# Decay between positions of a gated DeltaNet from differences of cumulative sums, in place of masked products and scans

## The chip, the cores and the metric

The kernel runs on one core of a Trainium2 chip. The metric is device time in microseconds (us) of one execution. The profile calls the engines PE (TensorE, matrix products), DVE (VectorE), ACT (ScalarE), POOL (GpSimd) and SP (SyncE, which here issues the transfers).

## What is computed

One layer of a streaming encoder block in float32: SEQ = 1024 positions, D_MODEL = 1024, batch 1. A modulated norm and one input projection feed a gated DeltaNet (8 heads of 128), a latent attention (8 heads) and branch gates; both are merged and projected, and a gated MLP with a short convolution follows. The change lies in the DeltaNet:

```python
gc = jnp.cumsum(chunks_s(g), axis=-1)
decay = jnp.exp(jnp.where(tri, gc[..., :, None] - gc[..., None, :], -jnp.inf))
a_mat = jnp.where(strict, jnp.einsum('bhncd,bhnjd->bhncj', k_beta, kc) * decay, 0.0)
...
intra = jnp.where(tri, jnp.einsum('bhncd,bhnjd->bhncj', qc, kc) * decay, 0.0)
k_dec = kc * jnp.exp(gc[..., -1:] - gc)[..., None]
```

`g` is at most 0, one number a position and head. Between two positions c and j of a chunk, what is remembered decays by exp(gc[c] - gc[j]), the exponential of the sum of g over the positions after j up to c. `a_mat` takes it where c > j, `intra` where c >= j.

## The kernel before

The kernel works in NB = 8 blocks of 128 positions, a head's decays being one tile G of 128x1024 (partition: position j of the block; columns: block and position c). Products on TensorE that must be exact are made as three passes over parts `_h` and `_l` of each operand.

The parts that matter here, in the order of time. Up to about 100 us inputs are normed and the first three heads of keys k0 to k2 are projected. Then, from 100 to 262 us, `k_dense` projects keys k3 to k7 (the loop over heads in `conv_proj`: tile `kNx` is the copy of the product out of PSUM, `kNa` the convolution of width 4, three scalar_tensor_tensor on VectorE at L402 and a SiLU on ScalarE), `decay_rates` computes g, beta and exponentials of its sums, and `k_post`, once for each head in two interleaved streams, transposes the keys (`kNt`, copied to `ktN` at L572), takes their norms (`sse`, `nrm`, `wst`, `nws`), calls `decay`, scales `kt` for the state update (`kdw`), stores it, and multiplies the Gram matrix kk by `nws` and G into `nB` (L591). `nB` is stored to DRAM (`bd_d`), and `inverse` loads all heads' diagonal blocks as X and inverts them in 62 pairs of VectorE instructions (L616, L618). Gate projections (`gt`, weights `gNw`, results `gst` through a sigmoid on ScalarE, L679) fill TensorE from about 200 us.

From 440 to 775 us the query heads follow. `d_prep` prepares a head: it calls `decay` again, and multiplies the Gram matrix kq by `wst` and G into `att`. `d_scan` runs the recurrence over the 8 blocks: ks (state times keys), R on VectorE (L795), y on TensorE and its copy on VectorE (L801), su and the new state S (L808, L810). From about 820 us on the attention, the merge and the MLP follow, without the decays.

`decay` as it stands: g of the head is sent to all partitions by a transfer, POOL multiplies by the mask m_gt (1 where c > j, else 0), VectorE sums along each block in 8 scans, ScalarE takes the exponential, and POOL masks the result, by m_gt for the keys and by m_ge (c >= j) for the queries. It is called 16 times. The tile G has one buffer in the query part; in the key part odd heads use the two buffers of another tag.

TensorE's order is fixed by `PEOrder`, a planner of streams with costs and due times; each product is pinned behind the one before. It gives the same order before and after, but for the one product on gT. All other engines' orders come from the scheduler of the Tile framework, which simulates the program; they are not written by hand. An engine runs its instructions in order.

Of the kernel before, what the change touches and what calls it, by code (L numbers as in the profile page):

```python
# [16 lines left out]
P = 128  # L17
# [97 lines left out]
def _body(tc, nc, ctx, A, out):  # L115
# [22 lines left out]
    def gtt(o, a, b, op):  # L138
        nc.gpsimd.tensor_tensor(o, a, b, op=op)  # L139
# [46 lines left out]


    ident = pc.tile([P, P], F32, name="ident")
    m_gt = pc.tile([P, P], F32, name="m_gt")
    m_ge = pc.tile([P, P], F32, name="m_ge")  # L190
    for m, pat, mul, cmp in ((ident, -1, 1, ALU.is_equal), (m_gt, 1, -1, ALU.is_gt), (m_ge, 1, -1, ALU.is_ge)):
        nc.gpsimd.memset(m, 1.0)
        nc.gpsimd.affine_select(out=m, in_=m, pattern=[[pat, P]], compare_op=cmp, fill=0.0, base=0,
                                channel_multiplier=mul)
    ones = pc.tile([P, P], F32, name="ones")
    nc.vector.memset(ones, 1.0)
# [261 lines left out]
    def bcast_row(src, n, name, pool_):  # L458
# [5 lines left out]
    hb = [P, NH, NB]  # L464
    beta, g, egc, negc, egl, nrm, wst, nws, sse = [
        po.tile(hb, F32, name=n) for n in ("beta", "g", "egc", "negc", "egl", "nrm", "wst", "nws", "sse")]
    g_d = dr.tile([NH, S], F32, name="g_d")

    def decay_rates():
        nea = bcast_row(A["dn_a_log"], NH, "nea", po)  # L470
        dtb = bcast_row(A["dn_dt_bias"], NH, "dtb", po)
        nc.scalar.activation(nea, nea, AF.Exp)
        yield ((("sm",),), 0.4)
        gs = po.tile([P, 5, NH, NB], F32, tag="sq", bufs=2, name="gs")
        al, e_, s_, z_, q_ = [gs[:, i] for i in range(5)]
        V = nc.vector
        V.tensor_tensor(al, albe[:, 0], dtb.unsqueeze(2).broadcast_to(hb), op=ALU.add)
        V.scalar_tensor_tensor(e_, al, -1.0, al, op0=ALU.mult, op1=ALU.min)
        nc.scalar.activation(e_, e_, AF.Exp)
        nc.scalar.activation(beta, albe[:, 1], AF.Sigmoid)  # L480
        V.tensor_scalar(s_, e_, 2.0, None, op0=ALU.add)
        V.reciprocal(s_, s_)
        V.tensor_tensor(s_, s_, e_, op=ALU.mult)
        V.tensor_tensor(z_, s_, s_, op=ALU.mult)
        V.tensor_scalar(q_, z_, 1.0 / 17.0, None, op0=ALU.mult)
        for d in (15, 13, 11, 9, 7, 5, 3):
            V.scalar_tensor_tensor(q_, q_, 1.0 / d, z_, op0=ALU.add, op1=ALU.mult)
        V.scalar_tensor_tensor(q_, q_, 1.0, s_, op0=ALU.add, op1=ALU.mult)
        V.tensor_scalar(al, al, 0.0, None, op0=ALU.max)
        V.scalar_tensor_tensor(q_, q_, 2.0, al, op0=ALU.mult, op1=ALU.add)  # L490
        V.scalar_tensor_tensor(g, q_, -1.0, nea.unsqueeze(2).broadcast_to(hb), op0=ALU.mult, op1=ALU.mult)
        gf = g.rearrange("p h b -> p (h b)")
        yield 8.0
        t = bank("tp", "gT")
        pe.tr(t[0:HB, 0:P], gf, ident)
        gT = po.tile([HB, P], F32, tag="sq", bufs=2, name="gT")
        nc.vector.tensor_copy(gT, t[0:HB, 0:P])
        nc.sync.dma_start(g_d.rearrange("h (b p) -> (h b) p", p=P), gT)
        t = bank("tp", "gcum")
        pe.mm(t[:, 0:HB], m_ge, gf)  # L500
        nc.scalar.activation(egc.rearrange("p h b -> p (h b)"), t[:, 0:HB], AF.Exp)
        V.tensor_scalar(negc, egc, -1.0, None, op0=ALU.mult)
        t = bank("tp", "gall")
        pe.mm(t[:, 0:HB], ones, gf)
        nc.scalar.activation(egl.rearrange("p h b -> p (h b)"), t[:, 0:HB], AF.Exp)
        pe.at[("g",)] = pe.t - CONV + 2.0

# [17 lines left out]
        nc.scalar.activation(sq, t, AF.Square)  # L525
        nc.vector.tensor_reduce(dst[:, hf * 4:hf * 4 + 4], sq.rearrange("p (j d) -> p j d", d=P), axis=AX.X, op=ALU.add)

    def decay(h, name, tag="G", bufs=1):
        G = po.tile([P, NB, P], F32, tag=tag, bufs=bufs, name=f"{name}G{h}")
        nc.sync.dma_start(G.rearrange("p b t -> p (b t)"), g_d[h:h + 1, :].broadcast_to([P, S]))  # L530
        gtt(G, G, m_gt.unsqueeze(1).broadcast_to([P, NB, P]), ALU.mult)
        for b in range(NB):
            nc.vector.tensor_tensor_scan(G[:, b, :], m_gt, G[:, b, :], 0.0, ALU.mult, ALU.add)
        nc.scalar.activation(G, G, AF.Exp)
        return G

    def mask_mul(G, m):
        gtt(G, G, m.unsqueeze(1).broadcast_to([P, NB, P]), ALU.mult)

    def gram(a, b, name):  # L540
        for hf in range(2):
# [21 lines left out]
    def k_post(par):  # L563
        for h in range(par, NH, 2):
            yield ((("k", h), ("g",)), CONV + 4.9 * h * (h < NS))
            kf = kfs[h]
            nc.sync.dma_start(kf_d[h], kf)
            kt = po.tile([P, NB, P], F32, tag="kd", bufs=2, name=f"kt{h}")

            def k_use(hf, t):  # L570
                sumsq(sse[:, h], hf, t, f"k{h}")
                nc.vector.tensor_copy(kt[:, hf * 4:hf * 4 + 4, :].rearrange("p j d -> p (j d)"), t)  # L572

            yield from tok_major(kf, f"k{h}", k_use)
            nc.vector.tensor_scalar(sse[:, h], sse[:, h], EPS, None, op0=ALU.add)
            nc.gpsimd.tensor_tensor(nrm[:, h], sse[:, h], phalf[:, 0:NB], op=ALU.pow)
            nc.vector.reciprocal(wst[:, h], sse[:, h])
            nc.vector.tensor_tensor(wst[:, h], wst[:, h], beta[:, h], op=ALU.mult)
            nc.vector.tensor_scalar(nws[:, h], wst[:, h], -1.0, None, op0=ALU.mult)
            G = decay(h, "k", *(("vn", 2) if h % 2 else ("G", 1)))  # L580
            kdw = po.tile([P, NB], F32, name=f"kdw{h}", tag="kdw", bufs=2)
            nc.vector.tensor_tensor(kdw, wst[:, h], G[:, :, P - 1], op=ALU.mult)
            gtt(kt, kt, kdw.unsqueeze(2).broadcast_to([P, NB, P]), ALU.mult)
            nc.sync.dma_start(kt_d[h], kt.rearrange("p b d -> p (b d)"))
            mask_mul(G, m_gt)
            nB = po.tile([P, NB, P], F32, tag="att", bufs=2, name=f"nB{h}")
            yield 4.0 if h < NS else 4
            for hf, t in gram(kf, kf, f"kk{h}"):
                for j in range(4):
                    b = hf * 4 + j  # L590
                    nc.vector.scalar_tensor_tensor(nB[:, b, :], t[:, j * P:(j + 1) * P], nws[:, h, b:b + 1], G[:, b, :],  # L591
                                                   op0=ALU.mult, op1=ALU.mult)
                yield
            for i in range(2):
                o = slice(i * 64, i * 64 + 64)
                nc.sync.dma_start(bd_d[h, :, i].rearrange("b j c -> j b c"), nB[o, :, o])
            nc.sync.dma_start(b12_d[h], nB[0:64, :, 64:128])
            pe.mark("pk", h)
# [117 lines left out]
    def d_prep():  # L716
        for h in range(NH):
# [48 lines left out]
                pe.mm(t[0:64, b * 64:b * 64 + 64], TW[64:128, b, :], U[64:128, b, 64:128])  # L766
            (nc.scalar.copy if 3 & 2 else nc.vector.tensor_copy)(U[0:64, :, 64:128], t[0:64, :].rearrange("p (b c) -> p b c", c=64))
            yield
            G = decay(h, "q")
            mask_mul(G, m_ge)  # L770
            att = d["att"] = po.tile([P, NB, P], F32, tag="att", bufs=2, name=f"att{h}")
            for hf, t in gram(kf, qf, f"kq{h}"):
                for j in range(4):
# [1055 lines left out]
```

## Time and profile before

| what | value |
|---|---|
| median of 3 runs (lowest to highest) | 2211.99 us (2209.98 to 2216.24) |
| profiled execution | 2214.16 us |
| its span, from first to last instruction | 2212.2 us |
| mean granted TensorE clock | 0.980 |
| busy: PE, DVE, ACT, POOL | 95%, 62%, 41%, 37% |

The profiled execution is 2.2 us above the median, and 1.96 us longer than its span. Shares of busy time are averages over stages with different limits; which engine an engine waits for in a stage is read from the waits and timelines there. The granted clock is 1.00 at 2.4 GHz and 0.50 at 1.2 GHz.

### The profile page before, as it was taken

The numbers are of one execution on the slowest core, as the hardware profiler recorded it, in microseconds if no ns is written. First come the engines' busy times: TensorE is split into PE (matmuls) and PEld (weight loads), VectorE is DVE, ScalarE is ACT, GpSimd is POOL, SyncE is SP. The second block draws the span as 40 slices with busy tenths as digits, with TensorE's granted clock in tenths as the row PEclk, the third lists the DMA queues.
The fourth block names the chain that finished last, engine by engine and source line by source line (L and its number), as shares of the span: only waits on it lengthen the run. The fifth ranks groups of instructions, "written<-read, shape, count | busy, mean of one in ns | idle before, by whom it ended". The sixth has DMA issues, their size and how long they took to land.

```text
span 2212.2 us, 30724 instructions
## 1 busy us (share of the span) xinstructions
PE 2093.9 (95%) x11525; PEld 1805.5 (82%) x11525; DVE 1377.9 (62%) x2212; ACT 902.4 (41%) x1822; POOL 812.4 (37%) x574
## 2 busy tenths in 40 slices
PE   7978899999999998899998999999999999999999
PEld 6866788878888898888877888898778888878887
DVE  7589499465555527658638886636575555555554
ACT  5644322463554522325324564236443333433221
POOL 1057420131212212427437770226554444442231
PEclk8989999999999999999999999999999999999999
DMA  9445633425223327578754446423322222244644
GB/s 281 125 137 155 168 112 90 138 76 154 91 86 102 99 77 240 175 247 285 240 153 138 121 119 204 148 77 115 115 96 86 86 82 81 96 144 146 219 143 147
DMA packets 277460, 309.30 MB, mean 140 GB/s; under 512 B 38895, under 2 KB 218428, under 8 KB 277056
## 3 DMA queue, kind: packets, MB, share of 16 engines
q1 hardware_dynamic: 277312, 307.35, 44.8%
q8 instruction: 90, 1.47, 0.3%
q14 instruction: 58, 0.48, 0.1%
HBM read 223.63 MB, written 83.66 MB: 139 GB/s over the span
## 4 chain that ended last, share of the span: by engine, by line
PE 60%; DVE 15%; DMA 7%; issue 3%; POOL 3%; ACT 2%; SPq 0%; POOLq 0%; ACTq 0%; DVEq 0%
PE d L63 11%; PE gt L63 5%; PE m L63 5%; PE my L63 4%; PE mx L63 4%; PE yb L63 4%; PE wo L63 4%; PE qt L63 3%; PE v L63 3%; PE q L63 3%; DVE lt L616 3%; DVE X L618 3%; PE s L63 2%; PE mz L63 2%; DMA wada<-in_w_ada 2%
## 5 line engine op out<-in xcount | busy, mean ns | idle before, releaser
L63 PE MATMUL d<-wd,gh 128*128 128x512 f32 x704 | 217.3, 390 | 2.2 <-DVE wd L151 1.7
L63 PEld LDWEIGHTS d<-wd,gh 128*128 128x128 f32 x704 | 132.1, 188 | 30.8 <-DVE wd L151 2.5
L63 PE MATMUL d<-wd,gl 128*128 128x512 f32 x352 | 137.0, 389 | 0.0
L139 POOL TENSOR_TENSOR wdr<-wdr,gf 128x512 f32<-128x512 f32 x44 | 68.8, 1565 | 164.0 <-DMA wdr<-in_ffn_w_down 157.6
L151 DVE TENSOR_TENSOR gl<-gr,gh 128x1024 fp32r<-128x1024 f32 x44 | 56.4, 1283 | 106.3 <-ACT gh L143 104.2
L143 ACT CAST gh<-gr 128x1024 fp32r<-128x1024 f32 x44 | 46.3, 1054 | 153.4 <-PE d L63 152.9
L63 PEld LDWEIGHTS d<-wd,gl 128*128 128x128 f32 x352 | 66.1, 188 | 13.8
L1236 ACT ACTIVATE P<-s,nm 128x512 f32<-128x512 f32 (+2 forms) x96 | 55.2, 581 | 51.7 <-DVE nm L1234 43.4
L136 POOL TENSOR_SCALAR P<-P,sm 128x896 f32<-128x896 f32 (+4 forms) x64 | 49.4, 780 | 63.1 <-DVE nm L1234 17.5
L139 POOL TENSOR_TENSOR acc<-acc,vv 128x512 f32<-128x512 f32 x44 | 64.5, 1486 | 20.0 <-ACT acc L1764 12.6
L616 DVE TENSOR_TENSOR lt<-X 128x62 f32<-128x62 f32 (+30 forms) x62 | 61.7, 996 | 9.1 <-issue 7.1
L151 DVE TENSOR_TENSOR wd<-wdr,wd 128x512 fp32r<-128x512 f32 x44 | 64.4, 1466 | 1.5 <-ACT wd L143 1.5
L1118 DVE SCALAR_TENSOR_TENSOR ada<-wada,sc,ada 128x1024 f32<-128x1024 f32 x28 | 41.5, 1481 | 35.3 <-DMA wada<-in_w_ada 35.1
L63 PE MATMUL mz<-T2h,wP 128*128 128x512 f32 x176 | 58.3, 392 | 3.2 <-ACT wP L143 2.1
L618 DVE TENSOR_TENSOR X<-X,lt 128x62 f32<-128x62 f32 (+30 forms) x62 | 59.5, 959 | 2.0
L1259 ACT CAST PTh<-pT 128x512 fp32r<-128x512 f32 (+2 forms) x96 | 45.9, 483 | 36.4 <-PE pT L66 36.0
L66 PE MATMUL pT<-ident,P 128*128 128x128 f32 x288 | 49.0, 280 | 11.2 <-DVE PTl L1260 8.2
L63 PE MATMUL m<-B21h,wP 128*128 128x512 f32 x176 | 58.9, 396 | 0.0
L63 PE MATMUL my<-T4h,wP 128*128 128x512 f32 x176 | 57.9, 390 | 0.9 <-DVE vv L1752 0.9
L63 PE MATMUL mx<-B22h,wP 128*128 128x512 f32 x176 | 57.9, 390 | 0.0
L63 PE MATMUL my<-T3h,wP 128*128 128x512 f32 x176 | 57.8, 389 | 0.0
L63 PE MATMUL m<-B11h,wP 128*128 128x512 f32 x176 | 57.5, 389 | 0.0
(1427 smaller groups left out, 7356.1 us busy)
## 6 DMA issues: line engine op xcount, KB each, us to landing
gr<-gg_d SPq DMA_DIRECT2D x44, 512.0 KB
wada<-in_w_ada SPq DMA_DIRECT2D x32, 512.0 KB
gg_d<-acc SPq DMA_DIRECT2D x22, 512.0 KB
wdr<-in_ffn_w_down SPq DMA_DIRECT2D x44, 256.0 KB
x<-in_x SPq DMA_DIRECT2D x16, 512.0 KB
ad<-in_w_ada SPq DMA_DIRECT2D x16, 512.0 KB
sg_d<-gst SPq DMA_DIRECT2D x32, 256.0 KB
q_d<-qst SPq DMA_DIRECT2D x48, 128.0 KB
```

The costliest lines, as they stand in the source:

```text
L63: self._pin(self.nc.tensor.matmul(out, lhsT, rhs, start=start, stop=stop, skip_group_check=more), cost)
L66: self._pin(self.nc.tensor.transpose(out=out, in_=in_, identity=ident), 0.107)
L136: return nc.gpsimd.tensor_scalar(o, i, by, 0.0, op0=ALU.mult, op1=ALU.add)
L139: nc.gpsimd.tensor_tensor(o, a, b, op=op)
L143: nc.scalar.copy(hi, src)
L151: return nc.vector.tensor_tensor(lo, src, hi.bitcast(F32), op=ALU.subtract)
L616: nc.vector.tensor_tensor(tv, X[:, 0:k, k:k + 1].broadcast_to([P, k, n]), X[:, k:k + 1, k + 1:64].broadcast_to([P, k, n]), op=ALU.mult)
L618: nc.vector.tensor_tensor(X[:, 0:k, k + 1:64], X[:, 0:k, k + 1:64], tv, op=ALU.add)
L1118: nc.vector.scalar_tensor_tensor(acc, raw, sc[:, k:k + 1], acc, op0=ALU.mult, op1=ALU.add)
L1236: nc.scalar.activation(Pt[:, kc], o, AF.Exp, bias=nm[:, 0:1], accum_out=sm[:, b:b + 1])
L1259: nc.scalar.copy(dh, tv)
```

## The change

g_d, from which the rows are sent to all partitions, now holds the cumulative sums: the product that made the transpose of g now has m_ge in place of the identity. A new tile `gc` holds the same sums by partition. `decay` subtracts gc of position j from the row and takes the minimum with a floor tile, in one scalar_tensor_tensor for each block on VectorE: `f_gt` is 0 where c > j and -10000 elsewhere, `f_ge` likewise for c >= j; after the exponential the masked places are 0. POOL's products with the masks and VectorE's scans go. The decay to a block's end, for `kdw`, comes from a new small tile `kde`, not from G's last column. `f_ge` lies in the tile `albe`, which is free by then; POOL fills it in two instructions.

```diff
--- before.py
+++ after.py
@@ -186,11 +186,12 @@
 
 
     ident = pc.tile([P, P], F32, name="ident")
-    m_gt = pc.tile([P, P], F32, name="m_gt")
+    f_gt = pc.tile([P, P], F32, name="f_gt")
     m_ge = pc.tile([P, P], F32, name="m_ge")
-    for m, pat, mul, cmp in ((ident, -1, 1, ALU.is_equal), (m_gt, 1, -1, ALU.is_gt), (m_ge, 1, -1, ALU.is_ge)):
-        nc.gpsimd.memset(m, 1.0)
-        nc.gpsimd.affine_select(out=m, in_=m, pattern=[[pat, P]], compare_op=cmp, fill=0.0, base=0,
+    for m, pat, mul, cmp, v_in, v_out in ((ident, -1, 1, ALU.is_equal, 1.0, 0.0), (f_gt, 1, -1, ALU.is_gt, 0.0, -1e4),
+                                          (m_ge, 1, -1, ALU.is_ge, 1.0, 0.0)):
+        nc.gpsimd.memset(m, v_in)
+        nc.gpsimd.affine_select(out=m, in_=m, pattern=[[pat, P]], compare_op=cmp, fill=v_out, base=0,
                                 channel_multiplier=mul)
     ones = pc.tile([P, P], F32, name="ones")
     nc.vector.memset(ones, 1.0)
@@ -464,6 +465,8 @@
     hb = [P, NH, NB]
     beta, g, egc, negc, egl, nrm, wst, nws, sse = [
         po.tile(hb, F32, name=n) for n in ("beta", "g", "egc", "negc", "egl", "nrm", "wst", "nws", "sse")]
+    gc, kde = [po.tile(hb, F32, name=n) for n in ("gc", "kde")]
+    f_ge = albe.rearrange("p a h b -> p (a h b)")
     g_d = dr.tile([NH, S], F32, name="g_d")
 
     def decay_rates():
@@ -492,16 +495,22 @@
         gf = g.rearrange("p h b -> p (h b)")
         yield 8.0
         t = bank("tp", "gT")
-        pe.tr(t[0:HB, 0:P], gf, ident)
+        pe.mm(t[0:HB, 0:P], gf, m_ge)
         gT = po.tile([HB, P], F32, tag="sq", bufs=2, name="gT")
         nc.vector.tensor_copy(gT, t[0:HB, 0:P])
         nc.sync.dma_start(g_d.rearrange("h (b p) -> (h b) p", p=P), gT)
         t = bank("tp", "gcum")
         pe.mm(t[:, 0:HB], m_ge, gf)
         nc.scalar.activation(egc.rearrange("p h b -> p (h b)"), t[:, 0:HB], AF.Exp)
+        nc.vector.tensor_copy(gc.rearrange("p h b -> p (h b)"), t[:, 0:HB])
         V.tensor_scalar(negc, egc, -1.0, None, op0=ALU.mult)
         t = bank("tp", "gall")
         pe.mm(t[:, 0:HB], ones, gf)
+        V.tensor_tensor(kde.rearrange("p h b -> p (h b)"), t[:, 0:HB], gc.rearrange("p h b -> p (h b)"), op=ALU.subtract)
+        nc.scalar.activation(kde, kde, AF.Exp)
+        nc.gpsimd.memset(f_ge, 0.0)
+        nc.gpsimd.affine_select(out=f_ge, in_=f_ge, pattern=[[1, P]], compare_op=ALU.is_ge, fill=-1e4, base=0,
+                                channel_multiplier=-1)
         nc.scalar.activation(egl.rearrange("p h b -> p (h b)"), t[:, 0:HB], AF.Exp)
         pe.at[("g",)] = pe.t - CONV + 2.0
 
@@ -525,17 +534,14 @@
         nc.scalar.activation(sq, t, AF.Square)
         nc.vector.tensor_reduce(dst[:, hf * 4:hf * 4 + 4], sq.rearrange("p (j d) -> p j d", d=P), axis=AX.X, op=ALU.add)
 
-    def decay(h, name, tag="G", bufs=1):
+    def decay(h, name, floor, tag="G", bufs=1):
+
         G = po.tile([P, NB, P], F32, tag=tag, bufs=bufs, name=f"{name}G{h}")
         nc.sync.dma_start(G.rearrange("p b t -> p (b t)"), g_d[h:h + 1, :].broadcast_to([P, S]))
-        gtt(G, G, m_gt.unsqueeze(1).broadcast_to([P, NB, P]), ALU.mult)
         for b in range(NB):
-            nc.vector.tensor_tensor_scan(G[:, b, :], m_gt, G[:, b, :], 0.0, ALU.mult, ALU.add)
+            nc.vector.scalar_tensor_tensor(G[:, b, :], G[:, b, :], gc[:, h, b:b + 1], floor, op0=ALU.subtract, op1=ALU.min)
         nc.scalar.activation(G, G, AF.Exp)
         return G
-
-    def mask_mul(G, m):
-        gtt(G, G, m.unsqueeze(1).broadcast_to([P, NB, P]), ALU.mult)
 
     def gram(a, b, name):
         for hf in range(2):
@@ -577,12 +583,11 @@
             nc.vector.reciprocal(wst[:, h], sse[:, h])
             nc.vector.tensor_tensor(wst[:, h], wst[:, h], beta[:, h], op=ALU.mult)
             nc.vector.tensor_scalar(nws[:, h], wst[:, h], -1.0, None, op0=ALU.mult)
-            G = decay(h, "k", *(("vn", 2) if h % 2 else ("G", 1)))
+            G = decay(h, "k", f_gt, *(("vn", 2) if h % 2 else ("G", 1)))
             kdw = po.tile([P, NB], F32, name=f"kdw{h}", tag="kdw", bufs=2)
-            nc.vector.tensor_tensor(kdw, wst[:, h], G[:, :, P - 1], op=ALU.mult)
+            nc.vector.tensor_tensor(kdw, wst[:, h], kde[:, h], op=ALU.mult)
             gtt(kt, kt, kdw.unsqueeze(2).broadcast_to([P, NB, P]), ALU.mult)
             nc.sync.dma_start(kt_d[h], kt.rearrange("p b d -> p (b d)"))
-            mask_mul(G, m_gt)
             nB = po.tile([P, NB, P], F32, tag="att", bufs=2, name=f"nB{h}")
             yield 4.0 if h < NS else 4
             for hf, t in gram(kf, kf, f"kk{h}"):
@@ -766,8 +771,7 @@
                 pe.mm(t[0:64, b * 64:b * 64 + 64], TW[64:128, b, :], U[64:128, b, 64:128])
             (nc.scalar.copy if 3 & 2 else nc.vector.tensor_copy)(U[0:64, :, 64:128], t[0:64, :].rearrange("p (b c) -> p b c", c=64))
             yield
-            G = decay(h, "q")
-            mask_mul(G, m_ge)
+            G = decay(h, "q", f_ge)
             att = d["att"] = po.tile([P, NB, P], F32, tag="att", bufs=2, name=f"att{h}")
             for hf, t in gram(kf, qf, f"kq{h}"):
                 for j in range(4):
```

The lists below print instructions in the order of an engine's program: line, operation, output, inputs, columns; head numbers stand in names (`kG1` is the key decay of head 1), the last number is the tile's own. Scans are printed as SCALAR_TENSOR_TENSOR too; line 533 tells them.

VectorE in the key part, around `nB` of head 1. Before:

```order
L582 TENSOR_TENSOR kdw1_1226<-wst_700,kG1_1214 128x8
L151 TENSOR_TENSOR k7w_l_1623<-k7w_r_1620,k7w_h_1622 128x1024
L578 TENSOR_TENSOR wst_700<-wst_700,beta_694 128x8
L402 SCALAR_TENSOR_TENSOR k4a_1348<-k4x_1091,v1_91,k4a_1348 128x1023
L579 TENSOR_SCALAR nws_701<-wst_700 128x8
L402 SCALAR_TENSOR_TENSOR k4a_1348<-k4x_1091,v1_91,k4a_1348 128x1022
L575 TENSOR_SCALAR sse_702<-sse_702 128x8
L402 SCALAR_TENSOR_TENSOR k4a_1348<-k4x_1091,v1_91,k4a_1348 128x1021
L577 RECIPROCAL wst_700<-sse_702 128x8
L591 SCALAR_TENSOR_TENSOR nB1_1231<-kk1_0_1296,nws_701,kG1_1214 128x128 x4
L591 SCALAR_TENSOR_TENSOR nB1_1231<-kk1_1_1305,nws_701,kG1_1214 128x128 x4
```

After:

```order
L588 TENSOR_TENSOR kdw1_1234<-wst_702,kde_706 128x8
L583 RECIPROCAL wst_702<-sse_704 128x8
L596 SCALAR_TENSOR_TENSOR nB1_1238<-kk1_0_1301,nws_703,kG1_1223 128x128 x3
L584 TENSOR_TENSOR wst_702<-wst_702,beta_696 128x8
L596 SCALAR_TENSOR_TENSOR nB1_1238<-kk1_0_1301,nws_703,kG1_1223 128x128
L596 SCALAR_TENSOR_TENSOR nB1_1238<-kk1_1_1310,nws_703,kG1_1223 128x128 x4
L151 TENSOR_TENSOR k7w_l_1624<-k7w_r_1621,k7w_h_1623 128x1024
L585 TENSOR_SCALAR nws_703<-wst_702 128x8
L578 COPY kt2_1254<-k2t0_1255 128x512
L578 COPY kt2_1254<-k2t1_1266 128x512
L588 TENSOR_TENSOR kdw2_1293<-wst_702,kde_706 128x8
L403 SCALAR_TENSOR_TENSOR k4a_1353<-k4x_1102,v1_93,k4a_1353 128x1023
```

`nB1` moved ahead of the weights' part `k7w_l` and of the convolution `k4a`; the copies `kt2`, which stood ahead of these rows before, now come behind `nB1`.

ScalarE between the keys' last projection and the first gate. Before:

```order
L534 ACT_TABLE_LOAD
L534 ACTIVATE kG7_1950<-kG7_1950 128x1024
L143 CAST g2w_h_2240<-g2w_r_2238 128x1024
L394 COPY k7x_1626<-k7_1_1653 128x512
L399 ACTIVATE k7a_1747<-k7x_1626,v1_91 128x1024
L404 ACT_TABLE_LOAD
L404 ACTIVATE k7a_1747<-k7a_1747 128x1024
L679 ACT_TABLE_LOAD
L679 ACTIVATE gst0_0_1784<-gt0_0_1759 128x512
```

After:

```order
L143 CAST g2w_h_2235<-g2w_r_2233 128x1024
L395 COPY k7x_1627<-k7_1_1654 128x512
L543 ACT_TABLE_LOAD
L543 ACTIVATE kG6_1819<-kG6_1819 128x1024
L400 ACTIVATE k7a_1746<-k7x_1627,v1_93 128x1024
L684 ACT_TABLE_LOAD
L684 ACTIVATE gst0_0_1783<-gt0_0_1758 128x512
```

The copy `k7x` and, further on, `gst0_0` now stand ahead of work that they stood behind: a table load with an exponential of a decay tile, and the SiLU on `k7a`.

VectorE in the query part, in block 1 of head 6, where the decays of head 7 are made. Before:

```order
L808 COPY S6_0_6052<-su6_0_6050 128x128
L795 SCALAR_TENSOR_TENSOR R6_1_6065<-ks6_1_6063,negc_697,vn6_5894 128x128
L533 SCALAR_TENSOR_TENSOR qG7_6313<-m_gt_74,qG7_6313 128x128 x8
L801 COPY y6_1_6092<-y6_1_6090 128x128
L840 TENSOR_TENSOR rq5_5492<-rq5_5492,oss5_6026 128x8
```

After:

```order
L812 COPY S6_0_6033<-su6_0_6031 128x128
L542 SCALAR_TENSOR_TENSOR qG7_6294<-qG7_6294,gc_705,albe_695 128x128 x8
L799 SCALAR_TENSOR_TENSOR R6_1_6046<-ks6_1_6044,negc_699,vn6_5877 128x128
L844 TENSOR_TENSOR rq5_5477<-rq5_5477,oss5_6007 128x8
L845 TENSOR_TENSOR on5_5544<-on5_5544,rq5_5477 128x1024
L805 COPY y6_1_6073<-y6_1_6071 128x128
```

The eight instructions on `qG7` moved from behind `R6_1` to ahead of it, and `rq5` and `on5` from behind the copy `y6_1` to ahead of it.

## Rows read from the trace of the kernel before

**Rows 1.** The page, part 1: each engine's busy time, its share and instructions.

```profile
...
PE 2093.9 (95%) x11525; PEld 1805.5 (82%) x11525; DVE 1377.9 (62%) x2212; ACT 902.4 (41%) x1822; POOL 812.4 (37%) x574
...
```

**Rows 2.** Stretches, TensorE alone: length, busy time (instructions), granted clock, DMA share, GB/s.

```profile
...
132.00:139.00 7.00, 3.83 (x14) 0.51 0.20 78
156.00:163.00 7.00, 4.30 (x18) 0.51 0.51 167
204.00:212.00 8.00, 4.18 (x17) 0.58 0.47 145
220.00:228.00 8.00, 6.22 (x15) 0.57 0.62 181
260.00:266.00 6.00, 5.50 (x17) 0.72 0.53 142
100.00:262.00 162.00, 131.05 (x641) 0.92 0.57 155
262.00:396.00 134.00, 132.62 (x577) 0.99 0.33 101
740.00:748.00 8.00, 5.63 (x22) 0.79 0.24 66
440.00:775.00 335.00, 319.69 (x1948) 0.99 0.34 101
850.00:1350.00 500.00, 461.04 (x3104) 0.97 0.59 184
...
```

**Rows 3.** Waits of TensorE from 100 to 300 us.

```profile
...
PE gt L63 <- ACT gst L679: 9.7, 3, 4.2
PE kk L63 <- DVE nB L591: 7.4, 2, 6.1
PE k2t L66 <- DVE kt L572: 7.0, 2, 5.1
PE gt L63 <- ACT k7x L394: 6.6, 1, 6.6
...
```

**Rows 4.** POOL by shape, 100 to 262 us: busy, mean ns, idle before.

```profile
...
L139 POOL TENSOR_TENSOR kG<-kG,m_gt 128x1024 f32<-128x1024 f32 x16 | 44.9, 2814 | 14.2 <-DMA kG<-g_d 14.2
L139 POOL TENSOR_TENSOR kt<-kt,kdw 128x1024 f32<-128x1024 f32 x8 | 18.1, 2258 | 15.0 <-DVE kdw L582 15.0
L576 POOL TENSOR_TENSOR nrm<-sse,phalf 128x8 f32<-128x8 f32 x8 | 14.4, 1796 | 18.7 <-DVE sse L575 15.2 <-DVE wst L578 3.4
...
```

**Rows 5.** VectorE by shape, same stretch and columns.

```profile
...
L533 DVE TENSOR_TENSOR_SCAN kG<-m_gt,kG 128x128 f32<-128x128 f32 x64 | 31.6, 557 | 0.0
L591 DVE SCALAR_TENSOR_TENSOR nB<-kk,nws,kG 128x128 f32<-128x128 f32 x64 | 17.2, 337 | 13.9 <-POOL kG L139 8.6 <-DMA z2w_r<-in_w_in 5.3
...
L487 DVE SCALAR_TENSOR_TENSOR gs<-gs 128x64 f32<-128x64 f32 x7 | 1.6, 225 | 0.2
...
L402 DVE SCALAR_TENSOR_TENSOR k4a<-k4x,v,k4a 128x1022 f32<-128x1022 f32 x1 | 1.3, 1282 | 0.0
...
```

**Rows 6.** Timeline of VectorE around 150 us: start, duration.

```profile
...
149.32 3.50 DVE L402 SCALAR_TENSOR_TENSOR k4a<-k4x,v,k4a 128x1023 f32<-128x1023 f32 x1
...
```

**Rows 7.** Timeline of POOL, the same time.

```profile
...
149.33 2.40 POOL L139 TENSOR_TENSOR kG<-kG,m_gt 128x1024 f32<-128x1024 f32 x1
```

**Rows 8.** Timeline of VectorE where its inverse chain begins.

```profile
...
252.55 2.63 DVE L533 TENSOR_TENSOR_SCAN qG<-m_gt,qG 128x128 f32<-128x128 f32 x8 [7.27 <-POOL qG L139]
262.25 0.22 DVE L616 TENSOR_TENSOR lt<-X 128x62 f32<-128x62 f32 x1 [7.07 <-issue]
...
```

**Rows 9.** Timeline of TensorE behind the inverse chain.

```profile
...
394.66 0.50 PE L63 MATMUL q<-hh,q1w_h 128*128 128x512 f32 x1 [0.79 <-ACT v0x L394]
...
```

**Rows 10.** Waits of TensorE from 440 to 775 us.

```profile
...
PE su L63 <- DVE y L801: 8.7, 5, 4.0
...
```

**Rows 11.** POOL by shape, 440 to 775 us.

```profile
...
L139 POOL TENSOR_TENSOR qG<-qG,m_gt 128x1024 f32<-128x1024 f32 x7 | 17.2, 2457 | 23.5 <-DMA qG<-g_d 17.3 <-DVE R L795 6.2
L139 POOL TENSOR_TENSOR qG<-qG,m_ge 128x1024 f32<-128x1024 f32 x7 | 17.1, 2443 | 31.6 <-ACT qG L534 31.6
...
```

**Rows 12.** VectorE by shape, 440 to 775 us.

```profile
...
L533 DVE TENSOR_TENSOR_SCAN qG<-m_gt,qG 128x128 f32<-128x128 f32 x56 | 23.1, 477 | 8.1 <-POOL qG L139 8.1
...
```

**Rows 13.** Timeline of VectorE in the last head of this part.

```profile
...
734.03 0.35 DVE L795 SCALAR_TENSOR_TENSOR R<-ks,negc,vn 128x128 f32<-128x128 f32 x1 [1.54 <-PE ks L63]
737.35 4.78 DVE L533 TENSOR_TENSOR_SCAN qG<-m_gt,qG 128x128 f32<-128x128 f32 x8 [2.97 <-POOL qG L139]
742.05 0.26 DVE L801 COPY y<-y 128x128 f32<-128x128 f32 x1
...
```

## The prediction

> **What bounds the kernel now.** I began with the page's busy line: TensorE works 2093.9 us, 95% of the span [rows 1]. A change to VectorE and GpSimd (POOL) can only win what TensorE waits, plus what it then runs at the lower clock. So I cut the span where the decays are made and read TensorE there [rows 2]. From 100 to 262 us, where the eight key heads are prepared, it is busy 131.05 of 162 us; from 262 to 396 it idles 1.4 us, while VectorE runs the inverse of the triangular blocks; from 440 to 775, the query heads, it idles 15.3 of 335. From about 820 us nothing of the change is left.
>
> The list of TensorE's waits gives the causes in the key part [rows 3]: it waits 7.0 us for copies of kt, 7.4 us for nB (6.1 of it once), 6.6 us for the copy k7x, and 9.7 us for gst: 30.7 of its 31 idle us. VectorE and ScalarE are late there, and what makes them late shows in the groups: 16 products of 128x1024 with the mask cost POOL 44.9 us, the 64 scans cost VectorE 31.6 us, and VectorE waits 8.6 us for POOL's masked G at nB alone [rows 4, 5]. The clock comes on top. In the five short stretches behind these waits the granted mean is 0.51 to 0.72, where full speed (2.4 GHz) is 1.00 and the lower level (1.2 GHz) 0.50. At a mean c, busy time times (1-c) would be saved: 3.83x0.49 + 4.30x0.49 + 4.18x0.42 + 6.22x0.43 + 5.50x0.28 = 1.9+2.1+1.8+2.7+1.5 = 10.0 us [rows 2]. All that the key part can give is thus 40.7 us.
>
> **What goes and what comes.** POOL loses 24 products with m_gt and 8 with m_ge: 44.9 us in the key part, 17.2+17.1 in seven query heads [rows 4, 11], and all are links of a chain (load, product, scans, exp, product, nB or att). VectorE loses 128 scans, 64 for 31.6 us and 56 of the rest for 23.1 [rows 5, 12]. It gets 128 scalar_tensor_tensor of the same size, both tensors in SBUF. No such row exists. Bounds: 225 ns (the same operation on 64 columns) and 337 ns (nB, 128 columns with one source in PSUM) [rows 5]. The slope from 64 to 1022 columns is (1282-225)/958 = 1.10 ns a column, so 128 columns give 225+64x1.10 = 295 ns; I take that. 64 of them are 18.9 us against 31.6: 12.7 us less in the key part, some 6 in the query part. The copy of gc, the subtraction and exp for kde (64 columns, some 0.2 us each by the 225 ns row) and the floor tile made once on POOL lie in the 14.2 us in which POOL waits for the first loads [rows 4]. Without that cover they would cost below 1.5 us, five small instructions of 0.2 to 0.3. The cumulative sum of gT is one matmul in place of a transpose: nothing.
>
> Why are 64 scans worth 31.6 us, at a mean of 557 ns against 477 in the query part? A timeline shows it on another instruction: the convolution step on k4a begins at 149.32 and takes 3.50 us, while POOL's masking runs from 149.33 to 151.73; its twin of one column less takes 1.28 [rows 6, 7, 5]. The 2.2 us of difference are POOL's instruction. By that row, 16 fewer POOL products mean up to 16 such delays fewer on VectorE. But 18.1 us of kt products and 14.4 of the nrm powers stay in the key part [rows 4] and can still hold up the new instructions, which read two SBUF tensors as the scans did. The Trainium skill has a rule for this (SBUF — State Buffer, "Who interferes with whom"): a VectorE instruction with two SBUF inputs and a GpSimd instruction that reads SBUF exclude each other for a whole instruction. The trace agrees (3.50 against 1.28 us). The rule speaks for the masks' removal, and against any hope that the new operation is free of such delays: should it meet POOL as often as the scans did, the time would be near that of the second rival below, 2198, where my sum says 2178.
>
> Now TensorE's waits, one by one, along the changed order.
> - kt of k1 and k2 and the first nB, 8.3 idle + 1.9 clock. The 24 decay steps of k0, k1, k3 that stand ahead of these copies shrink, and kt copies of k2 come later in the order, behind k1's nB. My walk leaves 3.5 us of idle time, with half the clock loss: gain 5.8.
> - nB of k1, 6.1 + 2.1. Before, it stands behind the lo part of k7's weights and the three steps on k4a, one of them the 3.50; now it is ahead of them, and its G needs no POOL. Gain 8.2.
> - k7x, 6.6 + 1.8. Before, ScalarE does a table load, an exp of G and a cast ahead of the copy; now the exp comes behind it. Gain 8.4.
> - gst, 9.7 + 4.2 (2.7 and 1.5). Before, gst of the first gate stands behind k7a's SiLU, which waits for VectorE's steps; now it is ahead. The two later ones stood behind exps of G that came late through POOL. Gain 13.9.
>
> That is 36.3. Against it stands that VectorE, not POOL, now waits in order for each G load, and POOL waited 14.2 us for two of them [rows 4]: I take 3 us off. **Key part: 33 us.**
>
> This holds only if the inverse chain, which VectorE starts at 262.25 after 7.07 us of idle time, begins as much earlier; TensorE waits only 0.79 us behind its end, so the two are level now [rows 8, 9]. The nB of k7 depends on the same shortened chain, and in SP's queue (read in the order, not shown) its store now stands ahead of a load of kdl, which before had to wait for a store of kt. So I let the chain move with TensorE.
>
> Query part: TensorE's largest idle item is 8.7 us for y, 4.0 of it once [rows 10]: y's copy stood behind eight scans, 737.35 to 742.05 [rows 13]. The load had landed a POOL product earlier, about 737.35-2.46 = 734.9. Now eight steps of 0.30 or less run from there to 737.2, ahead of R (it was at 734.03, so 3.2 later), but y's copy no longer has the scans ahead: about 739. Of 4.0 idle some 1.5 stay: 2.5 gained and the 1.2 of clock (5.63x0.21) [rows 2]. In the other heads VectorE takes over loads for which POOL waited 17.3 us [rows 11] while scans shrink: I put these at -0.7. **Query part: 3 us.**
>
> Behind that TensorE's work shifts as it stands. Sum: the profiled execution took 2214.16 us (span 2212.2 and 1.96 around it); less 33+3 it is **2178 us**. The median of the runs is 2.2 lower than that execution; the range covers this.
>
> **Rivals.**
> - *VectorE waits for G loads* (slower). Each of 16 loads now blocks everything behind it on VectorE: R, S and y of the running recurrence. In the key and query parts together all other gains are at most 36.3+6.7 = 43 us. A stall of 1 us costs 1.33 with its clock (10.0 to 30.7 above). Should 3.5 us a load (17.3 over 5 waits, [rows 11]) reach TensorE, that is 16x3.5x1.33 = 74: 2214+74-43 = 2245. It ties at 2.0 us a load and is slower by over 0.3% from 2.3. For it: in-order VectorE, one buffer for the query's G. Against: TensorE has projection work between two steps of a recurrence, and POOL's waits were mostly not TensorE's. Chance 0.06.
> - *Half a gain*: kt and nrm on POOL still hold up the new steps, or the inverse chain moves by only half and TensorE waits the rest behind it. Half of 33, and no query gain: 2198. For it: 32.5 us of POOL work stays [rows 4], and TensorE is level with the chain at 394.66. Against: the masking was the larger share, and 12.7 us leave VectorE. Chance 0.15.
> - *No change within 0.3%* (6.6 us, about what a measurement of this kernel can tell from no change): what is won comes back between 850 and 1350, where TensorE idles 39 us at a granted 0.97 [rows 2] and waits follow loads whose order may fall otherwise. Its work shifts with the rest, so I expect at most 5 either way. With a gain under 12, 2210. Chance 0.05.
> - *More*: all idle time and clock loss of both parts go: 40.7 + 15.3 + 1.2 = 57, 2157. Chance 0.06, nearly all of it short of that.
>
> The forecast, 2167 to 2190, has 0.68. The range of 2160 to 2199 takes in the half gain and most of the larger. Faster: 0.68+0.15+0.06 = 0.89; same 0.05; slower 0.06.
>
> **What would show it.** Right: TensorE idles under 8 us from 100 to about 225; the waits for nB, k7x and gst are gone; eight steps run in about 2 us; nB on VectorE no longer waits for POOL; the inverse begins near 225 and ends near 360 with TensorE behind it waiting under 3 us; y's longest wait is below 2. Wrong: waits of VectorE for G loads that turn up as TensorE's waits for R, S or kt; steps of over 400 ns in the mean; an inverse that starts after 235; idle time of well over 39 us in the gated part.

## The result and the profile after

The changed kernel takes 2182.01 us (median of 4 runs, 2181.25 to 2186.88) against 2212.32 of the kernel before: a ratio of 0.9861, 95% interval 0.9848 to 0.9874. It is faster by 30 us, where 36 were forecast, and lies inside the range of 2160 to 2199. Timed once more beside the kernel before, it was faster by 24 (2187.22 against 2211.44). The span of the profiled execution is 2180.2 us.

The page's busy line of the changed kernel:

```profile
...
PE 2085.7 (96%) x11526; PEld 1800.2 (83%) x11526; DVE 1334.7 (61%) x2214; ACT 903.8 (41%) x1822; POOL 735.2 (34%) x544
...
```

Against [rows 1], POOL loses 77 us of work (812.4 to 735.2) and VectorE 43 (1377.9 to 1334.7). TensorE has the same work; it is busy 8 us less, at a mean granted clock of 0.984 in place of 0.980. What counts is TensorE in its stretches (length, busy time, granted clock, DMA share, GB/s), as in [rows 2]:

```profile
...
100.00:262.00 162.00, 151.64 (x755) 0.97 0.62 172
262.00:396.00 134.00, 129.09 (x560) 0.97 0.39 122
440.00:775.00 335.00, 326.66 (x1949) 0.99 0.34 102
850.00:1350.00 500.00, 465.35 (x3052) 0.98 0.60 189
...
```

From 100 to 262 us it is busy for 151.64 us in place of 131.05, at a mean clock of 0.97 in place of 0.92. From 262 to 396 it idles 4.9 us where it had idled 1.4. From 440 to 775 it idles 8.3 in place of 15.3. The waits from 100 to 440 us, to hold against [rows 3], which end at 300 us (total, times, longest):

```profile
...
PE zt L63 <- ACT zst L684: 5.5, 2, 4.9
PE gt L63 <- ACT gst L684: 5.4, 1, 5.4
PE k3t L66 <- DVE kt L578: 2.7, 1, 2.7
PE k2t L66 <- DVE kt L578: 1.2, 1, 1.2
...
PE k1t L66 <- DVE kt L578: 0.5, 1, 0.5
```

The waits for nB and k7x are gone, those for kt are down to 4.4 us in three. One wait for gst is left, of 5.4 us, at another gate's product than the three from before; a wait of 4.9 us for zst is new. VectorE in the key part, which answers to [rows 5]:

```profile
...
L542 DVE SCALAR_TENSOR_TENSOR kG<-kG,gc,f_gt 128x128 f32<-128x128 f32 x64 | 17.6, 346 | 3.2 <-DMA kG<-g_d 3.1
L596 DVE SCALAR_TENSOR_TENSOR nB<-kk,nws,kG 128x128 f32<-128x128 f32 x64 | 17.3, 340 | 0.2
L584 DVE TENSOR_TENSOR wst<-wst,beta 128x8 f32<-128x8 f32 x8 | 3.3, 415 | 0.1
...
```

The 64 steps take 17.6 us where 64 scans took 31.6; nB costs the same but no longer waits for POOL (8.6 us before, now 0.2 for anything); even the small product on wst went from a mean of 907 ns (a row of that view that is not shown) to 415.

Where the new waits come from is seen in three timelines. VectorE:

```profile
...
215.81 1.40 DVE L542 SCALAR_TENSOR_TENSOR qG<-qG,gc,albe 128x128 f32<-128x128 f32 x5 [9.03 <-DMA qG<-g_d]
...
234.79 0.23 DVE L621 TENSOR_TENSOR lt<-X 128x62 f32<-128x62 f32 x1 [13.35 <-DMA X<-bd_d]
...
```

ScalarE, the same time:

```profile
...
215.78 1.28 ACT L543 ACT_TABLE_LOAD   x1 [8.75 <-DMA qG<-g_d]
218.71 1.06 ACT L543 ACTIVATE qG<-qG 128x1024 f32<-128x1024 f32 x1 [1.64 <-DVE qG L542]
...
222.01 1.09 ACT L684 ACTIVATE gst<-gt 128x512 f32<-128x512 f32 x2
```

TensorE:

```profile
...
222.66 0.79 PE L63 MATMUL gt<-hh,g2w_h 128*128 128x512 f32 x1 [5.42 <-ACT gst L684]
...
```

SyncE, where the load that they wait for is issued:

```profile
...
207.06 0.59 SPq L162 DMA_DIRECT2D z2w_r<-in_w_in  x1
207.69 1.65 SPq L540 DMA_DIRECT2D qG<-g_d  x1
...
```

The load of qG0, the first query head's decay, was issued at 207.69 behind a weight load and landed 8.1 us later. VectorE stood at the steps on qG0 for 9.03 us, with k7's copy, norm and nB behind them; ScalarE stood at the exponential for 8.75, with gst behind it; TensorE waited for gst. Because nB of k7 was late, the inverse began at 234.79, where about 225 was forecast.

In the kernel before, the last of the three waits for gst stood behind the same exponential, and POOL, ahead of it, behind the same load (from the timelines of SyncE, POOL, ScalarE and TensorE):

```profile
...
240.23 0.42 SPq L530 DMA_DIRECT2D qG<-g_d  x1
...
250.13 2.39 POOL L139 TENSOR_TENSOR qG<-qG,m_gt 128x1024 f32<-128x1024 f32 x1 [4.69 <-DMA qG<-g_d]
...
255.25 1.28 ACT L534 ACT_TABLE_LOAD   x1 [8.68 <-DVE qG L533]
...
260.50 0.50 PE L63 MATMUL gt<-hh,g3w_h 128*128 128x512 f32 x1 [3.73 <-ACT gst L679]
...
```

There the load took 9.9 us from its issue to POOL's start, and k7's copies and nB stood ahead of the scans on qG0 (nB at 243.12, the scans at 252.55). The change left the load in ScalarE's way, and it put VectorE's work for k7 behind it as well.

### The profile page after: what moved, and what is told of

Read it like the earlier page. It is cut to its first block, busy times and chain, and to the rows that moved or that the text cites. A ratio compares the mean times of both kernels' runs of the same rounds, so it can differ in the third digit from the quotient of the medians.

```text
span 2180.2 us, 30681 instructions
## 1 busy us (share of the span) xinstructions
PE 2085.7 (96%) x11526; PEld 1800.2 (83%) x11526; DVE 1334.7 (61%) x2214; ACT 903.8 (41%) x1822; POOL 735.2 (34%) x544
## 4 chain that ended last, share of the span: by engine, by line
PE 70%; DVE 13%; DMA 8%; issue 3%; ACT 3%; POOL 3%; SPq 1%; ACTq 0%; DVEq 0%; POOLq 0%
PE d L63 11%; PE gt L63 5%; PE m L63 5%; PE my L63 5%; PE mx L63 5%; PE yb L63 4%; PE v L63 4%; PE wo L63 4%; PE qt L63 4%; PE q L63 3%; PE s L63 3%; PE mz L63 2%; PE ya L63 2%; DMA wada<-in_w_ada 2%; PE zt L63 2%
```

## Experiments

Each kernel was timed beside the kernel before on one chip; the chip differs between some rows, so the ratio is what compares across rows. To see where a lead (how much earlier TensorE is than in the kernel before) is made or lost, the table gives the time at which TensorE starts a few products, taken from the first and last starts in the views of single tiles: the first product of z0 and of z5 (two gates' weights), the first and last product of y in the recurrence's output (at), and the first attention score (s).

| kernel | median us, ratio (95%) | z0 | z5 | first at | last at | first s |
|---|---|---|---|---|---|---|
| before | 2212.32 | 267.7 | 322.1 | 451.0 | 818.9 | 1139.3 |
| before again | 2211.36, 1.0002 (0.9989 to 1.0016) | 270.1 | 324.5 | 454.3 | 823.0 | 1134.3 |
| changed | 2182.01, 0.9861 (0.9848 to 0.9874) | 241.8 | 302.1 | 431.3 | 792.1 | 1103.7 |
| changed again | 2187.22, 0.9886 (0.9868 to 0.9904) | 241.0 | 302.5 | 432.1 | 799.7 | 1110.6 |
| masks back | 2201.83, 0.9952 (0.9938 to 0.9967) | 258.8 | 320.4 | 448.8 | 812.9 | 1126.0 |
| scans, no masks | 2195.70, 0.9940 (0.9919 to 0.9961) | 246.9 | 308.2 | 439.2 | 804.0 | 1115.5 |
| copies on VectorE | 2186.16, 0.9889 (0.9865 to 0.9913) | 240.7 | 295.1 | 430.9 | 795.4 | 1109.2 |
| first query decay late | 2180.82, 0.9877 (0.9856 to 0.9898) | 233.5 | 294.3 | 427.9 | 791.9 | 1103.5 |
| both of these | 2177.12, 0.9848 (0.9830 to 0.9866) | 231.3 | 285.7 | 424.7 | 786.4 | 1100.0 |
| new keys only | 2192.14, 0.9919 (0.9902 to 0.9935) | 241.4 | 304.9 | 436.0 | 803.4 | 1114.8 |
| new queries only | 2211.09, 0.9997 (0.9983 to 1.0011) | 263.8 | 323.9 | 453.3 | 817.1 | 1128.6 |
| both, query steps later | 2164.26, 0.9787 (0.9769 to 0.9805) | 230.5 | 284.9 | 422.7 | 773.2 | 1085.7 |
| query steps later alone | 2172.61, 0.9814 (0.9796 to 0.9832) | 243.3 | 304.6 | 433.0 | 783.6 | 1097.8 |
| both, without the copies | 2167.51, 0.9806 (0.9785 to 0.9827) | 228.3 | 289.9 | 423.2 | 773.8 | 1087.1 |

Executions already differ at the start of the key part: TensorE's first product there (k3) lies between 102.3 and 105.9 us in these profiles, so a difference of 3 us in a row of the table is no finding.

### Masks or scans

```diff
...
+one = ones.unsqueeze(1).broadcast_to([P, NB, P])
+gtt(G, G, one, ALU.mult)
 for b in range(NB):
     nc.vector.scalar_tensor_tensor(G[:, b, :], ...)
 nc.scalar.activation(G, G, AF.Exp)
+gtt(G, G, one, ALU.mult)
```

> The changed kernel with POOL's two products of 128x1024 put back into each decay, by a tile of ones (before the eight steps and after the exponential), so that the numbers stay as they are: the scans' saving alone is left. Theory A (the gain is the POOL products: two links in each chain, and instructions that hold up VectorE): most of the gain goes, 2200 to 2215 us. Rival B (the gain is the shorter VectorE instruction): most of it stays, 2183 to 2192.

```diff
 # in the kernel before
-gtt(G, G, m_gt.unsqueeze(1).broadcast_to([P, NB, P]), ALU.mult)
 ...
-mask_mul(G, m_gt)
 ...
-mask_mul(G, m_ge)
```

> The kernel before without its 32 mask products on POOL; the scans stay, so the decays at masked places are not those of the reference. Theory A: most of the gain is there, 2182 to 2192 us, the new operation giving at most 5 us. Rival B: most is missing, 2200 to 2212.

Masks back: 2201.83, in theory A's bracket; about 10 of the 30 us stay (a ratio of 0.9952). Scans without masks: 2195.70, between the two brackets; the masks' removal alone gives 13 by its ratio of 0.9940. Neither alone is most of the whole, so both theories fall as they were put. At z0, though, at the end of the key part, A is near right: without masks 20.8 of the 25.9 us are there, with them 8.9. VectorE in the key part, masks back:

```profile
...
L544 DVE SCALAR_TENSOR_TENSOR kG<-kG,gc,f_gt 128x128 f32<-128x128 f32 x64 | 29.9, 529 | 2.1 <-POOL kG L139 2.1
L599 DVE SCALAR_TENSOR_TENSOR nB<-kk,nws,kG 128x128 f32<-128x128 f32 x64 | 17.2, 337 | 5.2 <-POOL kG L139 5.1
L587 DVE TENSOR_TENSOR wst<-wst,beta 128x8 f32<-128x8 f32 x8 | 7.3, 913 | 0.1
...
```

Scans without masks:

```profile
...
L532 DVE TENSOR_TENSOR_SCAN kG<-m_gt,kG 128x128 f32<-128x128 f32 x64 | 22.7, 426 | 5.6 <-DMA kG<-g_d 5.6
...
```

The same 64 steps take 29.9 us with POOL's products beside them and 17.6 without; the scans take 31.6 with [rows 5] and 22.7 without. So the new operation is cheaper by 5.1 us, and POOL's products cost VectorE 9 to 12 us on these instructions alone, besides what they cost the small ones (wst 913 ns in the mean against 415). How much of the masks' 13 us is this, and how much the two links that they add to each chain, no run separates. nB, which has one tensor in PSUM, takes 337 to 341 ns in all of them. This is the rule of the Trainium skill that the prediction cited (SBUF — State Buffer, "Who interferes with whom"), now with the same instruction on both sides of it.

### Where the key part's lead went

```diff
-(nc.scalar.copy if r % 2 else nc.vector.tensor_copy)(XT, ...)
+nc.vector.tensor_copy(XT, ...)
```

> The changed kernel with the four transposed copies XT of the inverse that ScalarE makes moved to VectorE. In the changed kernel TensorE waits 4.91 us at 302 us for zst, which stands behind such a copy on ScalarE, which waits 12.76 us for VectorE's inverse. Theory C (this in-order wait eats 7 us of the key part's gain, 4.9 and some 2 of clock): 2174 to 2178 us and no wait at zt. Rival D (the inverse chain is the bound there, so that the wait only moves to what follows it): 2180 to 2184, with a new wait of TensorE between 340 and 400 us.

```diff
+ins =
 nc.vector.scalar_tensor_tensor(G[:, b, :], G[:, b, :], gc[:, h, b:b + 1], floor, ...)
+if name == "q" and h == 0:
+    follow(ins, last_nB[NH - 1], True)   # behind k7's last nB on VectorE
```

> The changed kernel with the eight steps on qG0, the decay of the first query head, held behind the last nB on VectorE. In the changed kernel VectorE waits 9.03 us and ScalarE 8.75 us for the load of qG0, and TensorE 5.42 us for gst behind it. Theory E (an in-order wait for a G load, as the slower rival had it, eats 5.4 us and some 2 to 3 of clock, and delays the inverse by some 9): 2172 to 2177 us. Rival F (the time comes back at the next wait, zt at 302 or the load of X): 2179 to 2184.

> The changed kernel with both edits: the inverse's copies XT on VectorE, and the first query head's decay behind the last nB. Alone, the first moved TensorE's wait of 4.9 us from zt to 4.2 us at q1 behind the inverse chain; the second started that chain 7.9 us earlier but met the old wait at zt. Theory G (two links in series, each hiding the other): TensorE is 28 to 33 us ahead of the kernel before at the first at (19.7 in the changed kernel), and the time is 2170 to 2176 us. Rival H (the lead is lost in the query part or behind it whatever comes before): 2179 to 2184.

> The kernel with the query steps later and the first query head's decay late, but with the inverse's copies XT on ScalarE as in the changed kernel. Theory P (behind the inverse chain TensorE waits in any case, so that edit is worth under 3 us): 2162 to 2168 us. Rival Q (the wait at zt costs its full 5 us and its clock): 2169 to 2173.

In the changed kernel ScalarE's copy of the inverse's result stands ahead of zst, and waits for VectorE:

```profile
...
300.50 1.08 ACT L628 COPY XT<-X 128x512 f32<-128x512 f32 x1 [12.76 <-DVE X L623]
301.48 0.60 ACT L684 ACTIVATE zst<-zt 128x512 f32<-128x512 f32 x1
...
```

With these copies on VectorE, z5 starts 7 us earlier (295.1 against 302.1; the start at k3 was 2.8 earlier by itself), and nothing of it is left at the first at. TensorE's waits from 300 to 440 us in that kernel:

```profile
...
PE q L63 <- ACT v0x L395: 4.2, 1, 4.2
PE zt L63 <- ACT zst L684: 1.7, 1, 1.7
...
```

The 4.2 us at q1 are the old 0.79 at the same place [rows 9], grown. There q1 waits for a copy on ScalarE, behind q0's SiLU, behind q0's convolution, which stands at the end of VectorE's inverse chain. Rival D's mechanism holds: the chain is the bound. The time, 2186.16, is 2 us above its bracket and, by the ratio, with the changed kernel's two. The other edit moves the chain's start. VectorE with the first query decay late:

```profile
...
211.04 2.16 DVE L600 SCALAR_TENSOR_TENSOR nB<-kk,nws,kG 128x128 f32<-128x128 f32 x8 [2.35 <-PE kk L63]
215.77 2.19 DVE L544 SCALAR_TENSOR_TENSOR qG<-qG,gc,albe 128x128 f32<-128x128 f32 x8 [2.58 <-DMA qG<-g_d]
226.94 0.22 DVE L625 TENSOR_TENSOR lt<-X 128x62 f32<-128x62 f32 x1 [8.97 <-DMA X<-bd_d]
...
```

nB of k7 now precedes the steps on qG0 and the inverse begins at 226.94, 7.85 us earlier; z0 starts at 233.5 in place of 241.8. At the first at 3.4 of these 8.3 us are left, the old wait at zt being there still, and in time the kernel is not told from the changed one (2180.82, in rival F's bracket). Theory E's mechanism is shown and its price was too high. Both edits together bring the first at to 424.7, 26.3 and 29.6 us ahead of the two profiles of before where theory G had 28 to 33, and 6.6 us earlier than in the changed kernel, of which 2.4 are a start that was earlier by itself (k3 at 103.4 and 105.8), and TensorE again waits at q1, 4.1 us. The time of 2177.12 lies between the two brackets. The last run leaves the copies as changed, with the query edit of the next section: 2167.51 against 2164.26, in theory P's bracket and with intervals that overlap. What the copies' place is worth is thus under what can be told; what the chain's start is worth, some 4 us at the first at.

### The query part

> The changed kernel with the old operations (two POOL products and eight scans) in the query heads, on the new tile of sums, so the queries' decays are not those of the reference; the key part is as changed. In the changed kernel TensorE's lead grew by 7.1 us from the first to the last at. Theory I (the query part gained these 7, twice what the prediction gave it): the lead stays as it is at the first at, and the time is 2186 to 2191 us. Rival J (these 7 are not the decays' but the order around them): 2180 to 2185.

> The changed kernel with the old operations in the key heads, on the new tile of sums, so the keys' decays are not those of the reference; the query part is as changed. Theory I: the lead at the first at is 0 to 4 us, it grows by 7 to the last at and by some 5 behind it through another order of loads: 2197 to 2203 us. Rival J: 2203 to 2211.

```diff
 # in the kernel with both edits
-if name == "q" and h == 0:
-    follow(ins, last_nB[NH - 1], True)
+if name == "q":
+    follow(ins, last_rec[-min(7, len(last_rec))] if h else last_nB[NH - 1], True)
 # last_rec: VectorE's instructions on R, y and S, as they are written
```

> The kernel of both edits, with the eight steps of the query heads 2 to 7 also held back on VectorE, by some 10 to 40 instructions, to behind a later step of the running recurrence, when their load has long landed. In the changed kernel TensorE waits 3.9 us for S and 2.7 for R in the query part, where these instructions stand behind steps that wait for a load. Theory K (the in-order wait for a load is what is left there): 4 to 6 us less than with both edits alone, and less than 3 us of waits for S and R. Rival L (the exponential then comes late for att, and the wait moves there): the same or slower, with waits for att or for what is behind it on VectorE.

> The changed kernel with only the eight steps of query heads 2 to 7 held back behind a later step of the recurrence; the first query head's decay and the inverse's copies stay as changed. Theory K (the in-order wait for the loads costs the query part some 11 us, independently of the key part): 2167 to 2173 us, and a lead that grows by 16 to 19 us from the first to the last at. Rival M (holding back pays only together with the two other edits): 2177 to 2183.

> The changed kernel once more, unaltered, beside the others on one chip. Both theories: 2179 to 2185 us; what differs from its first trace (the start of the key part, the lead at each stage) is what one execution differs from another.

From first to last at, the kernel before takes 367.9 and 368.7 us in its two profiles, and the one with new keys only 367.4. The changed one takes 360.8 and 367.6, and the four other kernels with its query steps (copies on VectorE, first query decay late, both of these, new queries only) 361.7 to 364.5. So the query part gains between 0.3 and 7.9 us, 3.4 to 7.0 in those four, and the 7 us of theory I are near the upper end.

In time the new queries alone give nothing (2211.09, at the upper end of rival J's bracket), and the new keys alone give 18 us (2192.14, a little above theory I's), where both give 24 to 30. Some 6 to 12 us thus come only with both. A part of them is seen: the decay of the first query head is made in the key part, and with its scans and POOL products there the inverse begins at 237.66, 2.9 us later than in the changed kernel, and the first at some 4 us later. The rest stays open. The waits of TensorE in the query part, changed kernel, first profile:

```profile
...
PE ks L63 <- DVE S L812: 3.9, 4, 2.2
PE y L63 <- DVE R L799: 2.7, 1, 2.7
PE su L63 <- DVE y L805: 0.9, 1, 0.9
...
```

Second profile:

```profile
...
PE ks L63 <- DVE S L812: 6.4, 5, 3.7
PE y L63 <- DVE rq L844: 3.3, 1, 3.3
PE y L63 <- DVE R L799: 2.4, 1, 2.4
...
```

The long waits for y of before, 8.7 us behind scans [rows 10], are gone in both, and waits for S and R have come, of a size that differs from one execution to the next. The four other kernels are like the second profile (4.3 to 4.9 us for S, 2.7 to 3.2 behind rq). VectorE's row in the first:

```profile
...
L542 DVE SCALAR_TENSOR_TENSOR qG<-qG,gc,albe 128x128 f32<-128x128 f32 x48 | 13.4, 345 | 11.9 <-DMA qG<-g_d 11.9
...
```

It waits 11.9 us for loads at these steps, where POOL had waited 17.3 [rows 11]; and now S and R stand behind them. With the steps of heads 2 to 7 held back to a place where the load has long landed (the edit names head 1 too, whose steps stay where they were and wait 1.0 us), VectorE:

```profile
...
L545 DVE SCALAR_TENSOR_TENSOR qG<-qG,gc,albe 128x128 f32<-128x128 f32 x48 | 13.2, 345 | 0.0
...
```

TensorE's waits there:

```profile
...
PE y L63 <- DVE R L804: 0.7, 1, 0.7
...
PE su L63 <- DVE y L810: 0.4, 1, 0.4
```

And its stretches, from 100 to 262 and from 440 to 775 us:

```profile
...
100.00:262.00 162.00, 157.63 (x788) 0.99 0.65 181
...
440.00:775.00 335.00, 332.84 (x2037) 1.00 0.34 106
...
```

TensorE is busy for 332.84 of 335 us. The query part takes 350.5 us, and the same in the two other kernels with this edit (350.6 and 350.6): 17 to 18 less than before, 10 to 17 less than in the changed kernel. The first and last starts of at, from the tile's views (kernel before, changed, and with the query steps later):

```profile
...
L63 PE MATMUL at<-y,att x128: 271/275/416, 451.0 to 818.9; 128*128 128x128 f32 x128
...
L63 PE MATMUL at<-y,att x128: 271/275/275, 431.3 to 792.1; 128*128 128x128 f32 x128
...
L63 PE MATMUL at<-y,att x128: 271/275/275, 422.7 to 773.2; 128*128 128x128 f32 x128
...
```

Theory K holds, at 12.9 us in time (2177.12 to 2164.26) where 4 to 6 were expected. The edit also lets the scheduler place other instructions anew, which no run holds fixed; but the waits that go are those for S, R and rq. Alone the edit brings the changed kernel to 2172.61, inside theory K's bracket. The changed kernel's own second timing on that chip is 2187.22, 2 us above what had been expected of it. With both edits of the key part it is 2164.26, the fastest of this study.

### The stage behind

> The kernel before, unaltered, profiled once more. From TensorE's last at to its first s the profiled execution of before took 320.1 us, and the changed kernel and all ten others 309.7 to 313.9, among them two with the same order of transfers there as before. Theory N (that execution was slow there by itself): 310 to 315 us in this one. Rival O (something of the old decays reaches that stage): 318 to 322.

From the last at to the first s, by the table, the first profile of before took 320.4 us and this one 311.3, like all changed ones (310.9 to 314.2). Theory N holds. That profile was 9 us slow in a stage that the change doesn't reach, and 3 to 4 us fast ahead of it. The difference of the two single traces (spans of 2212.2 and 2180.2 us) would put 9 of its 32 us there.

## Why the prediction was right, and where not

**What bounds the kernel** held: VectorE's and POOL's work counts only through TensorE's waits. 120 us of work went and the time fell by 24 to 30.

**The price of the steps** was 18.9 us for 64; they took 17.6. The masks' share and the operation's (8.9 and 5.1 of the 14.0 us) are as the argument from [rows 6, 7] had it: most of what was saved had been lost to POOL. That the sum came out is in part luck. Its bounds of 225 and 337 ns are means of single records, and the steps' mean, 346 ns, lies above both; 64 times 346 ns is 22.1 us, and the busy time is less because the records of successive steps overlap.

**The key part, 33 us**, was mis-sized. Up to the third gate (g2, 240.2 and 244.0 us in the two profiles of before, 211.5 and 211.7 changed) the lead is 28 to 33 us; the terms for kt, nB, k7x and the first gst came to about 31. What failed is the last item of the fourth term and the step behind it. Of the 13.9 us for gst, the 3.7 with their clock did not come: a gst waits 5.4 us in their place, behind the same exponential of qG0. The prediction put its lateness on POOL, but POOL had itself waited 4.69 us for the load of qG0, and the change does nothing to the load. And "I let the chain move with TensorE" was wrong: the chain began 27.5 us earlier, not 37, because VectorE stood 9 us at that same load, and at the first at 19 to 23 us are left of the 33. Three us had been taken off for VectorE's waits on loads; the mechanism was named, the one place where it mattered was not. The order showed it, where the steps on qG0 stand ahead of k7's second kt copy, and so did the trace of before, where this load took 9.9 us.

**The query part, 3 us**, holds as a sum (0.3 to 7.9, and mostly somewhat more than 3), from two larger terms: y's waits gone, and VectorE's waits for loads come.

**The slower rival** had the right mechanism and came part of the way. Held back, the steps save 10 to 17 us over six loads, clock and all: 1.7 to 2.9 us a load. The tie was put at 2.0 us a load without the clock, or 2.7 with it, for all 16, against 43 us of other gains; of these, 6.7 are the query part's, for which the terms there give only 3.7. It did not decide since the key part's loads hardly wait: VectorE idles 3.2 us ahead of all 64 steps there. **Half a gain** did not happen by its reason, POOL's remaining work, but the bound at the inverse chain that it names as well did take part of the gain. **Behind 820 us** little came or went: from the last at to the end of the span it is 1386.2 us before (second profile), 1388.1 and 1388.4 changed.

**Its signs** came in part. Eight steps took 2.2 us, the waits for nB and k7x went, y's longest wait (that of su) was 0.9 us, and TensorE did not wait at q1 behind the chain. But TensorE idled 9.8 us from 100 to 225, not under 8; gst still waited; the chain ended at 369.8, not near 360; and one sign of being wrong was there, VectorE's waits for G loads turning up as TensorE's for R and S (2.7 and 3.9 us).

That the forecast of 2178 was so near is luck in part, for misses offset each other: 10 to 14 us too much in the key part, up to 5 too little in the query part, and some 3 us by which before's profiled execution stood above its later timings.

## What to carry to other kernels

A product on POOL beside VectorE work on two SBUF tensors cost twice here, in its own chain and in what it held up; removing it can be worth more than a cheaper instruction on VectorE (here 13 us alone against 10). When a load's first reader moves to a busier engine, ask for each load what stands behind that reader: the wait that POOL could afford stopped the recurrence on VectorE, and placing the reader 5 to 31 us later took 13 to 15 us off, half of what the change itself gave. A lead counts only where the next chain in series (here the inverse on VectorE) starts earlier too.

## What was not expected of the hardware

The load of qG0, 512 KB written from one row of 4 KB, took 8.1 us from issue to landing while a weight load and stores were under way, and 9.9 in the kernel before; six loads of the same size in the query part of the changed kernel, for which VectorE waited, took 3.6 to 5.0. Single executions of one kernel differed by 9 us in one stage and made up most of it in others, with medians of all runs within 0.1% (2212.32 and 2211.36).
